# Other starting addresses for the operands of a sub-layer's products

## The chip, the cores and the metric

The kernel runs on one core of a Trainium2 chip, in one launch. The metric is the device time of an execution in microseconds (us); the median of three runs stands for a kernel. A profile is one more execution, recorded by the hardware profiler. "Busy" is the time in which an engine executes; the span is the time from the first to the last instruction on the core.

## The reference: what is computed

A two-layer diffusion backbone over 512 latent tokens and 256 context tokens, model width 1024, all in 32-bit floats. Each layer is a feed-forward half step, a token mixer (a short convolution in the first layer, grouped attention in the second), and another feed-forward half step:

```python
def swiglu(h, w_in, w_out):
    gate, up = jnp.split(h @ w_in, 2, axis=-1)
    return (jax.nn.silu(gate) * up) @ w_out
...
        h = norm_modulate(x_lat, norm_g[i, 2], m_lat[:, 2, 0], m_lat[:, 2, 1])
        x_lat = x_lat + MACARON_WEIGHT * m_lat[:, 2, 2] * swiglu(h, ffn_w_in[i, 1], ffn_w_out[i, 1])
        if not last:
            hc = norm_modulate(x_ctx, norm_g[i, 2], m_ctx[2, 0], m_ctx[2, 1])
            ...
    return rms_norm(x_lat, final_g)
```

`w_in` is 1024 x 5632 and `w_out` is 2816 x 1024. The second half step of the last layer (in the kernel `ffn(gp, 1, 2, "end", ...)`, the "last feed-forward sub-layer") works on the 512 latent tokens alone, since nothing reads the context tokens any more; all earlier sub-layers work on 768.

## The kernel before

**Splitting.** Every number that goes into a matmul is split into a high part (rounded by a ScalarE copy to the float type that TensorE takes at full pace) and a low part (what is left, a VectorE subtraction); `split`, L204 to L206. A product is then three matmuls, in this order: high weights by high operand (L876), high weights by low operand (L877), low weights by high operand (L878). This is the helper `mm3`. Every matmul loads its own weights of 128 x 128 beside the one before it.

**The seven products.** The input projection of a feed-forward sub-layer goes column by column: 22 columns of 128 gate and 128 up units. The first two columns are multiplied directly, gate and up, half of the tokens at a time (`directly`, L1106). The other 20 use Strassen's scheme on 2 x 2 blocks: tokens in two halves, the inner dimension in two halves, gate and up as the two rows. It takes seven block products M1 to M7 (`PRODUCTS`, L65) instead of eight, each over four chunks of 128 of the inner dimension: 4 x 3 matmuls (`product`, L1134). The weight combinations are formed by VectorE as they are needed (`add_product`, L384), split, and put into one of eight granules ahead of TensorE, or of some extra places.

**The operands T.** The moving operands of the products are eight pairs of tiles: the four blocks of the normalized input, B11, B21, B12, B22, and four combinations, T1 to T4. Each tile holds four rows of as many columns as there are tokens in a half: 384 in the earlier sub-layers, 256 in the last. The opening of a sub-layer (`opening`, L765) writes them: `early`, `parted` (L808) and `sum_parted` (L838), in program order on hooks between the matmuls of the sub-layer before and of the first columns. `t_tiles` (L748) makes the pair of a name.

**Slots.** Fourteen slots in SBUF, `T0` to `T13`, of 4 x 384 numbers (6144 bytes a partition), four of them with two more columns a row (386, for the first sub-layer's bias columns) and small tiles behind them, hold the T tiles in turn with other things: weight tiles, attention operands. A small tile `shift` of 24 numbers at the head of the constants and pads behind the wide slots set where the slots begin: in the program as built, every slot, every weight tile and every other matmul operand used here begins 96 bytes past a multiple of 256. In the last sub-layer a tile takes 4096 bytes of its slot, from the slot's first byte. Its slots are listed by

```python
LAST_T_SLOTS = {"B11": (0, 1), "B21": (2, 3), "B12": (6, 7), "T4": (6, 7), "T1": (8, 13), "B22": (9, 10), "T2": (11, 12), "T3": (4, 5)}
```

high part first. `geo` holds the halves' width and the slot table in force; before the last sub-layer it is set to 256 columns and this table (L1829).

**Order.** TensorE's and SyncE's instructions run in the order of the program text. The hooks, and in some regions a kept program order, set that of VectorE and ScalarE. Output products (`out_steps`) follow after every four columns: 512 columns wide, operands gh and gl.

Of the kernel before, what the change touches and what calls it, by code (L numbers as in the profile page):

```python
# [26 lines left out]
NH = NT // 2  # L27
# [47 lines left out]
HELD_AFTER_T = ((6, 7), (10, 11), (8, 9))  # L75

LAST_T_SLOTS = {"B11": (0, 1), "B21": (2, 3), "B12": (6, 7), "T4": (6, 7), "T1": (8, 13), "B22": (9, 10), "T2": (11, 12), "T3": (4, 5)}
LAST_F_SLOTS = {(0, 0): 4, (1, 0): 5, (0, 1): 11, (1, 1): 12}
HELD_AFTER_LAST_T = ((8, 13), (11, 12), (9, 10))
HELD_AFTER_HEADS = ((6, 7), (9, 10))  # L80
# [53 lines left out]
def backbone(ctx: ExitStack, tc: tile.TileContext, a: dict, out: bass.AP):  # L134
# [42 lines left out]
    vec, at = {}, 0  # L177
# [23 lines left out]
    def slot(n, shape, name, dt=F32R):  # L201
        return xp.tile([P, *shape], dt, name=name, tag=f"T{n}")
# [407 lines left out]
    hh, hl = [None] * KC, [None] * KC  # L610
# [125 lines left out]
    T, full = {}, {}  # L736
    geo = SimpleNamespace(tokens=TOKENS, half=NH, groups=BOTH, t_slots=T_SLOTS, f_slots=F_SLOTS)
# [8 lines left out]
        region.pop().close()  # L746

    def t_tiles(name, more=0):  # L748
        T[name] = [slot(n, [4, geo.half + more], f"t{name}{z}") for n, z in zip(geo.t_slots[name], "hl")]

    def t_split(name, src, ks, pinned=False):
        split(T[name][0][:, ks], T[name][1][:, ks], src[:, ks], pinned)
# [12 lines left out]
    def opening(i, s):  # L765
# [27 lines left out]
        def early(half):  # L793

            t_tiles(f"B{half + 1}1")
            off, n = geo.tokens[0]
            for k, (hi, lo) in enumerate(zip(*([t[:, k, :] for k in range(4)] for t in T[f"B{half + 1}1"]))):
                m = 4 * half + k
                scale = scl[:, m, LAT : LAT + 1]
                act.activation(hi, xs(m, off, n), AF.Copy, scale=scale)  # L800
                dve.scalar_tensor_tensor(out=lo, in0=xs(m, off, n), scalar=scale, in1=hi.bitcast(F32), op0=ALU.mult, op1=ALU.subtract)  # L801
# [6 lines left out]
        def parted(half, tok, p, which="both", more=0):  # L808
            name = f"B{half + 1}{tok + 1}"
            if p == 0 and which != "lo":  # L810
                t_tiles(name, more)
            hi, lo = T[name][0][:, PAIRS[p], : geo.half], T[name][1][:, PAIRS[p], : geo.half]
            src = full[half, tok][:, PAIRS[p]]
            if which != "lo":
                act.activation(hi, src, AF.Copy)
            if which != "hi":
                dve.tensor_tensor(out=lo, in0=src, in1=hi.bitcast(F32), op=ALU.subtract)
# [20 lines left out]
        def sum_parted(which, p, pinned=False):  # L838
            if p == 0:
                t_tiles(which)  # L840
            t_split(which, full[which] if which in full else full[0, 0], PAIRS[p], pinned)
# [984 lines left out]
    with tc.tile_pool(name="g1", bufs=1) as gp:  # L1826
        stage["ssq"] = lambda: gp.tile([P, NT], F32, name="ssq", tag="ssq")
        heads = attention(gp, 1, 1)
    geo.__dict__.update(tokens=HALVES, half=NL // 2, groups=((0, NL),), t_slots=LAST_T_SLOTS, f_slots=LAST_F_SLOTS)  # L1829
    op4 = opening(1, 2)  # L1830
# [79 lines left out]
```

## Time and profile before

| what | value |
|---|---|
| median of three runs | 2400.55 us (2399.58 to 2401.14) |
| the profiled execution | 2400.25 us |
| its span | 2398.4 us |
| mean granted TensorE clock | 0.998 |
| TensorE matmuls busy | 2377.5 us (99%), 14303 |
| weight loads busy | 2252.4 us (94%) |
| VectorE busy | 2031.9 us (85%) |
| ScalarE busy | 1166.3 us (49%) |
| last sub-layer, from its first opening writes to the end | about 2030 to 2398 us |

A matmul's recorded duration runs from its start until its last result is written, so the durations of successive matmuls overlap; the pace is the distance from one start to the next.

### The profile page before, as it was taken

Reading aid. Unit: us, or ns where it says so; the run is one execution under the profiler, and the core shown is the slowest. Engines: PE = TensorE matmul, PEld = TensorE weight load, DVE = VectorE, ACT = ScalarE, POOL = GpSimd, SP = SyncE. Lnnn points to the kernel's source line nnn. Section 1 sums busy time; section 2 is a strip of 40 time slices with the busy share of each in tenths; the row PEclk is TensorE's granted clock in tenths of the full one; section 3 lists DMA queues with packets and bytes.
Section 4 is the critical chain, followed back from the end, with each engine's and each line's share of the span. In section 5 each row is a group of like instructions: output and inputs, shape, how many; then the busy total and the mean of one; then the engine's idle time right before and its main releaser. Section 6 shows DMA issues by size and latency. Waiting matters only on the chain.

```text
span 2398.4 us, 37639 instructions
## 1 busy us (share of the span) xinstructions
PE 2377.5 (99%) x14303; PEld 2252.4 (94%) x14303; DVE 2031.9 (85%) x4018; ACT 1166.3 (49%) x2198; POOL 135.4 (6%) x256
## 2 busy tenths in 40 slices
PE   9999999999999999999999999999999999999998
PEld 6999999999999999999999999999998889999998
DVE  6989989978988888888877988788778987987777
ACT  5634334355535553443435544343356776555555
POOL 0001111100000001000000001101100000000000
PEclk9999999999999999999999999999999999999999
DMA  9234444430334123323432144444441101233331
GB/s 337 86 113 139 129 127 131 129 115 27 107 105 132 40 70 116 119 95 117 128 105 67 51 130 129 142 139 120 136 132 54 45 10 58 70 121 96 99 106 62
DMA packets 93062, 253.71 MB, mean 106 GB/s; under 512 B 10320, under 2 KB 18640, under 8 KB 92880
## 3 DMA queue, kind: packets, MB, share of 16 engines
q1 hardware_dynamic: 71984, 183.65, 23.7%
q0 software_dynamic: 20352, 67.12, 9.5%
q8 instruction: 112, 1.84, 0.3%
q14 instruction: 70, 0.57, 0.1%
q10 hardware_dynamic: 544, 0.52, 0.1%
HBM read 249.16 MB, written 2.10 MB: 105 GB/s over the span
## 4 chain that ended last, share of the span: by engine, by line
PE 91%; DVE 4%; ACT 3%; DMA 1%; issue 1%; SPq 0%; DVEq 0%; ACTq 0%
PE ps_A L876 16%; PE ps_A L877 16%; PE ps_A L878 16%; PE ps_C L877 11%; PE ps_C L878 11%; PE ps_C L876 11%; PE ps_B L878 3%; PE ps_B L877 3%; PE ps_B L876 3%; PE ps_T L1557 1%; DVE f L778 0%; DMA ada<-in_ada_w 0%; DMA raw<-in_ffn_w_in 0%; ACT pr L1540 0%; PE ps_O L878 0%
## 5 line engine op out<-in xcount | busy, mean ns | idle before, releaser
L205 ACT ACTIVATE w<-raw 128x512 fp32r<-128x512 f32 (+1 forms) x862 | 522.4, 619 | 713.6 <-PE ps_A L878 222.6
L206 DVE TENSOR_TENSOR w<-raw,w 128x512 fp32r<-128x512 f32 (+1 forms) x862 | 574.0, 678 | 120.0 <-ACT w L205 106.3
L525 POOL DMA_DIRECT2D aw<-in_ada_t x240 | 129.4, 539 | 1367.0 <-DVE mods L546 968.5
L389 DVE TENSOR_TENSOR raw<-raw,raw 128x512 f32<-128x512 f32 x264 | 181.4, 688 | 10.0 <-DMA raw<-in_ffn_w_in 6.0
L877 PE MATMUL ps_C<-gl,w 128*128 128x512 f32 (+1 forms) x548 | 188.3, 344 | 0.0
L876 PE MATMUL ps_C<-gh,w 128*128 128x512 f32 (+1 forms) x548 | 188.1, 343 | 0.0
L878 PE MATMUL ps_C<-gh,w 128*128 128x512 f32 (+1 forms) x548 | 188.0, 343 | 0.0
L876 PE MATMUL ps_A<-gh,w 128*128 128x512 f32 (+1 forms) x540 | 185.5, 344 | 0.6 <-DVE x L944 0.6
L877 PE MATMUL ps_A<-gl,w 128*128 128x512 f32 (+1 forms) x540 | 185.6, 344 | 0.0
L878 PE MATMUL ps_A<-gh,w 128*128 128x512 f32 (+1 forms) x540 | 185.4, 343 | 0.0
L546 DVE CUSTOM_DVE_ANT_0 ps_S<-aw,silu_row,packed 128x512 f32<-128x512 f32 x208 | 156.8, 754 | 2.1 <-DMA aw<-in_ada_t 0.8
L546 DVE CUSTOM_DVE_ANT_0 ps_S<-aw,silu_row,mods 128x512 f32<-128x512 f32 x208 | 156.7, 753 | 1.0
L944 DVE SCALAR_TENSOR_TENSOR x<-ps_C,gat,x 128x512 f32<-128x512 f32 (+1 forms) x158 | 99.4, 630 | 44.0 <-PE ps_C L878 43.6
L876 PE MATMUL ps_A<-tB11h,w 128*128 128x384 f32 (+1 forms) x400 | 129.6, 324 | 0.2 <-ACT tB11h L800 0.2
L877 PE MATMUL ps_A<-tB11l,w 128*128 128x384 f32 (+1 forms) x400 | 129.3, 323 | 0.2 <-DVE tB11l L801 0.2
L878 PE MATMUL ps_A<-tB11h,w 128*128 128x384 f32 (+1 forms) x400 | 129.2, 323 | 0.0
L878 PE MATMUL ps_C<-tB22h,w 128*128 128x384 f32 (+2 forms) x376 | 121.6, 323 | 0.0
L877 PE MATMUL ps_C<-tB22l,w 128*128 128x384 f32 (+2 forms) x376 | 121.4, 323 | 0.0
L876 PE MATMUL ps_C<-tB22h,w 128*128 128x384 f32 (+2 forms) x376 | 121.3, 323 | 0.0
L944 DVE SCALAR_TENSOR_TENSOR x<-ps_A,gat,x 128x512 f32<-128x512 f32 (+1 forms) x162 | 101.7, 637 | 16.6 <-PE ps_A L878 16.4
L876 PEld LDWEIGHTS ps_A<-gh,w 128*128 128x128 f32 x540 | 102.2, 189 | 14.1 <-issue 1.0
L878 PEld LDWEIGHTS ps_C<-gh,w 128*128 128x128 f32 x548 | 103.8, 189 | 12.3
(486 smaller groups left out, 6938.7 us busy)
## 6 DMA issues: line engine op xcount, KB each, us to landing
raw<-in_ffn_w_in SPq DMA_DIRECT2D x170, 512.0 KB, 3.7
aw<-in_ada_t POOLq DMA_DIRECT2D x240, 256.0 KB, 2.9
raw<-in_ffn_w_out SPq DMA_DIRECT2D x80, 512.0 KB, 3.9
raw<-in_conv_w_in SPq DMA_DIRECT2D x24, 512.0 KB, 3.6
ada<-in_ada_w SPq DMA_DIRECT2D x28, 256.0 KB, 5.3
raw<-in_attn_w_qkv SPq DMA_DIRECT2D x12, 512.0 KB, 4.7
raw<-in_ada_w SPq DMA_DIRECT2D x8, 512.0 KB, 6.6
silu_row<-in_crow POOLq DMA_DIRECT2D x8, 512.0 KB, 4.1
```

The source lines that it names most:

```text
L205: hi = act.activation(dsth, src, AF.Copy)
L206: lo = dve.tensor_tensor(out=dstl, in0=src, in1=dsth.bitcast(F32), op=ALU.subtract)
L389: dve.tensor_tensor(out=quad(o), in0=quad(x), in1=quad(y), op=ALU.subtract)
L525: nc.gpsimd.dma_start(w, a["ada_t"][t, kh, j])
L546: ins = dve.tensor_tensor_reduce(out=junk, in0=w, in1=silu_row[kh][:, v, :], scale=1.0, scalar=total if kh else ada_b[:, i, hm // 2, col : ...
L876: pe.matmul(ps, wh, xh, start=first, stop=False, **kw)
L877: pe.matmul(ps, wh, xl, start=False, stop=False, **kw)
L878: pe.matmul(ps, wl, xh, start=False, stop=last, **kw)
L944: dve.scalar_tensor_tensor(out=x, in0=p[:, o - off : o - off + w], scalar=gat[:, m, v : v + 1], in1=x, op0=ALU.mult, op1=ALU.add)
L1557: pe.transpose(pt[:, c, :], pr[:, (c0 + c) * P : (c0 + c + 1) * P], ident)
```

## The change

The T tiles of the last sub-layer begin later in their slots: the high part's tile 32 numbers (128 bytes) and the low part's 16 numbers (64 bytes) after the slot's first byte. The tile is made flat, that much longer, and the view that the rest of the program uses leaves the first numbers out. Rows follow each other as before, 256 numbers each. Slots, instructions and their order, and the tiles of all other sub-layers (`geo.half == NH`) stay as they are.

```diff
 LAST_T_SLOTS = {"B11": (0, 1), "B21": (2, 3), "B12": (6, 7), "T4": (6, 7), "T1": (8, 13), "B22": (9, 10), "T2": (11, 12), "T3": (4, 5)}
+LAST_T_STARTS = (32, 16)
 LAST_F_SLOTS = {(0, 0): 4, (1, 0): 5, (0, 1): 11, (1, 1): 12}
...
     def t_tiles(name, more=0):
-        T[name] = [slot(n, [4, geo.half + more], f"t{name}{z}") for n, z in zip(geo.t_slots[name], "hl")]
+        if geo.half == NH:
+            T[name] = [slot(n, [4, geo.half + more], f"t{name}{z}") for n, z in zip(geo.t_slots[name], "hl")]
+            return
+        T[name] = []
+        for n, z, at in zip(geo.t_slots[name], "hl", LAST_T_STARTS):
+            t = slot(n, [at + 4 * geo.half], f"t{name}{z}")
+            T[name].append(t[:, at:].rearrange("p (k c) -> p k c", k=4))
```

## The prediction

> **What bounds the kernel now.** I read the page's busy times and its chain first, then a table of busy times by stretch around the last feed-forward sub-layer, then single matmuls in order of time.
>
> ```profile
> PE 2377.5 (99%) x14303; PEld 2252.4 (94%) x14303; DVE 2031.9 (85%) x4018; ACT 1166.3 (49%) x2198; POOL 135.4 (6%) x256
> PE 91%; DVE 4%; ACT 3%; DMA 1%; issue 1%; SPq 0%; DVEq 0%; ACTq 0%
> ```
>
> TensorE is busy 99% of the span and holds 91% of the chain that ended last. A busy TensorE need not be at its peak, so the question is at what pace the matmuls follow each other where the changed tiles are read. The table (columns: stretch, its length, busy us and instructions of PE, PEld, DVE, ACT and POOL, granted clock, DMA share, GB/s):
>
> ```profile
> 2036.00:2062.50 26.50, 26.00 (x212) 25.27 (x211) 24.25 (x50) 17.44 (x37) 0.00 (x0) 1.00 0.09 32
> 2062.50:2087.00 24.50, 22.89 (x140) 19.97 (x139) 24.07 (x45) 12.15 (x29) 0.00 (x0) 1.00 0.25 86
> 2087.00:2300.00 213.00, 213.00 (x1520) 201.71 (x1520) 176.14 (x319) 115.38 (x235) 0.00 (x0) 1.00 0.34 108
> ```
>
> Until about 2087 us the sub-layer opens behind VectorE (24.07 of 24.50 us busy in the second row). From 2087 on TensorE has no idle time at all (213.00 of 213.00), at a granted clock of 1.00. There every nanosecond of the pace counts.
>
> Starts of single matmuls (columns: start us, duration us, engine, line, output<-inputs), 256, 384 and 512 columns wide:
>
> ```profile
> 2144.73 0.28 PE L876 MATMUL ps_B<-tB21h,w 128*128 128x256 f32 x1
> ...
> 2145.93 0.28 PE L877 MATMUL ps_A<-tT3l,w 128*128 128x256 f32 x1
> ```
>
> ```profile
> 571.05 0.33 PE L876 MATMUL ps_B<-tB12h,w 128*128 128x384 f32 x1
> ...
> 573.13 0.33 PE L876 MATMUL ps_B<-tB12h,w 128*128 128x384 f32 x1
> ```
>
> ```profile
> 2199.82 0.39 PE L877 MATMUL ps_A<-gl,w 128*128 128x512 f32 x1
> ...
> 2202.09 0.39 PE L878 MATMUL ps_A<-gh,w 128*128 128x512 f32 x1
> ```
>
> Ten matmuls of 256 columns lie between the first pair: 1.20 us, 120 ns each. Twelve of 384: 2.08 us, 173.3 ns each. Ten of 512: 2.27 us, 227 ns each. From 256 to 384 columns the step is 53.3 ns for 128 columns, 0.417 ns a column; what is left over is 13.3 ns at each width (120 - 106.7, 173.3 - 160, 227 - 213.3). So each matmul takes its columns plus a constant 13.3 ns, the time of 32 columns, that is of 128 bytes of a moving row. The stretch from 2087 to 2300 agrees: of its 1520 matmuls 288 are the output products of 512 columns (six groups of 48) and 1232 are of 256, and 288 x 0.227 + 1232 x 0.120 = 213.2 us against 213.00.
>
> ```profile
> L877 PE MATMUL ps_C<-gl,w 128*128 128x512 f32 x48 | 18.7, 390 | 0.0
> ```
>
> This 13.3 ns is the only thing in the stage that the address of a moving operand could touch.
>
> **The change part by part.** No instruction, wait or DMA is added, taken away or put elsewhere; nothing is moved past a queue. The tiles T of the last sub-layer keep their slots, and what changes is where inside its slot a tile begins: high parts 128 bytes further, low parts 64. In the program as built every slot begins 96 bytes past a multiple of 256, and so does every weight tile. Afterwards high parts begin 224 past it, low parts 160. Modulo 128 the high parts stay at 96 and the low parts go to 32; modulo 64 nothing changes.
>
> *The writes.* Eight tile pairs, two halves each: 16 ScalarE copies and 16 VectorE subtractions write at the new addresses. The trace has the same writes with rows 8 bytes out of step (the first sub-layer's tB12 and tB22 have two more columns a row) beside rows in step (tB11, tB21):
>
> ```profile
> L817 DVE TENSOR_TENSOR tB11l<-f,tB11h 128x768 fp32r<-128x768 f32 x2 | 1.9, 960 | 1.0 <-ACT tB11h L815 1.0
> L817 DVE TENSOR_TENSOR tB12l<-f,tB12h 128x768 fp32r<-128x768 f32 x2 | 1.9, 956 | 0.1
> L815 ACT ACTIVATE tB11h<-f 128x768 fp32r<-128x768 f32 x2 | 1.7, 848 | 0.1
> L815 ACT ACTIVATE tB12h<-f 128x768 fp32r<-128x768 f32 x2 | 1.7, 846 | 0.2 <-DVE f L789 0.2
> ```
>
> 960 against 956 and 848 against 846 ns: at most 4 ns apart in either direction, so 32 writes are worth -0.1 to +0.1 us. I take 0. If the cover were gone (they feed the opening, which VectorE sets) that 0.1 us would be the whole cost.
>
> *The reads.* The sub-layer has 22 columns, 2 of them multiplied directly and 20 by seven products of 4 x 3 matmuls: 20 x 84 = 1680 matmuls of 256 columns read the T tiles, and the direct columns 192 more. The 192 and about one column's 84 run before 2087 us, where VectorE sets the pace and a TensorE that is faster only waits; about 1600 count. One nanosecond on each is 1.6 us.
>
> Does the pace depend on the address? Within what the trace holds, not on the slot. The tiles named below lie in different slots, at different distances from their weights and from their low parts, and each has the same median, 283 ns:
>
> ```profile
> L878 PE MATMUL ps_A<-tB11h,w x76: 282/283/283, 2036.8 to 2298.7; 128*128 128x256 f32 x76
> L876 PE MATMUL ps_C<-tB22h,w x64: 283/283/287, 2053.0 to 2297.0; 128*128 128x256 f32 x64
> L876 PE MATMUL ps_A<-tT3h,w x60: 283/283/283, 2081.2 to 2291.2; 128*128 128x256 f32 x60
> ```
>
> But all of them begin at 96 modulo 256. The one case off it is the first sub-layer's tB22, whose four rows begin 0, 8, 16 and 24 bytes further along:
>
> ```profile
> 121.21 0.33 PE L876 MATMUL ps_C<-tB22h,w 128*128 128x384 f32 x1
> 121.38 0.33 PE L877 MATMUL ps_C<-tB22l,w 128*128 128x384 f32 x1
> ...
> 122.25 0.33 PE L876 MATMUL ps_C<-tB22h,w 128*128 128x384 f32 x1
> 122.42 0.33 PE L877 MATMUL ps_C<-tB22l,w 128*128 128x384 f32 x1
> 122.59 0.34 PE L878 MATMUL ps_C<-tB22h,w 128*128 128x384 f32 x1
> 122.77 0.34 PE L876 MATMUL ps_C<-tB22h,w 128*128 128x384 f32 x1
> ...
> 123.12 0.34 PE L878 MATMUL ps_C<-tB22h,w 128*128 128x384 f32 x1
> 123.30 0.34 PE L876 MATMUL ps_A<-tB11h,w 128*128 128x384 f32 x1
> ```
>
> These twelve take 2.09 us against 2.08 in step, 0.8 ns more a matmul; the row at 16 bytes goes at 0.17 us a matmul, and the last, at 24 bytes, takes 0.53 us for three (177 ns each, 3.4 above 173.3). So the address does matter, at the scale of some bytes. The matmul that follows another width also leaves the pace:
>
> ```profile
> 182.91 0.28 PE L876 MATMUL ps_A<-gh,w 128*128 128x256 f32 x1
> 183.03 0.28 PE L877 MATMUL ps_A<-gl,w 128*128 128x256 f32 x1
> 183.14 0.28 PE L878 MATMUL ps_A<-gh,w 128*128 128x256 f32 x1
> 183.26 0.28 PE L876 MATMUL ps_A<-gh,w 128*128 128x256 f32 x1
> ...
> 2245.35 0.40 PE L876 MATMUL ps_C<-gh,w 128*128 128x512 f32 x1
> 2245.58 0.40 PE L877 MATMUL ps_C<-gl,w 128*128 128x512 f32 x1
> 2245.82 0.39 PE L878 MATMUL ps_C<-gh,w 128*128 128x512 f32 x1
> ...
> 2246.51 0.39 PE L878 MATMUL ps_A<-gh,w 128*128 128x512 f32 x1
> ```
>
> The first three after 182.91 need 0.35 us, not 0.36; the five from 2245.35 to 2246.51 need 1.16, not 1.135 (5 ns more each). After a few both fall back to the constant pace. I read that as follows: the start of a read is held to some regular beat, and the beat is short enough that 256, 384 and 512 columns all end on the same place in it. A shift by a whole number of beats then changes nothing. All widths seen are multiples of 128 columns, so the rows leave open whether the beat is 128 bytes (32 columns, the 13.3 ns) or a part of it, 64 or 32; a beat of 32 or 64 bytes makes both new starts neutral. That rows 16 and 24 bytes out already differ (0.52 us for three, from 122.25 to 122.77, against 0.53) speaks for a beat well below 128 bytes. That is inference, and it is where I choose.
>
> Bounds for the reads: from below, two of three matmuls lose half of the constant (6.7 ns), 1600 x 2/3 x 6.7 = -7.1 us; from above the same with the other sign, +7.1 us, which is the size of the dearest row out of step (3.4 ns on each, 5.4 us) and of the disturbed 512s (5 ns, 8 us). Near to neither, I take 0, as for all slots.
>
> Sum: 0 (instructions) + 0 (writes) + 0 (reads) on the profiled execution's 2400.25 us (span 2398.4 and 1.85 around it), which is 0.3 us under the median of the runs, 2400.55. **Forecast: 2400.3 us, no change**, its own range 2397 to 2404.
>
> The Trainium skill, TensorE: Matmul & The Clock Gate, section Back-to-back issue gap, gives N / 2.4 + 2.5 ns between matmuls, 109 ns for 256 columns where this trace shows 120 in each of some thousand; by that rule 10.8 ns of the 13.3 is not owed to the matmul itself, and if the new starts removed that, 1600 x 10.8 = 17 us, the sum would be 2383. The trace nowhere reaches that pace at 256 columns, and the section's own sustained figures lie off the formula too; it only makes the last case of the first rival below less absurd.
>
> **The rivals.** *Faster, by a half turn.* If the beat is 128 bytes, a matmul over a low part begins 64 bytes off from the high one before it, and the next high one again. The 32 columns' wait would become 16 in two of each three (high to low and low to high; high to high, with the next weights, keeps 32). -7.1 us: 2393.2. VectorE could follow: it is busy 19.42 of 20.00 us where products run, and would have 19.26, but makes weight parts up to eight ahead and has 13.33 of 20.00 in the output stretches.
>
> ```profile
> 2100.00:2120.00 20.00, 20.00 (x169) 20.00 (x168) 19.42 (x38) 14.21 (x32) 0.00 (x0) 1.00 0.41 136
> 2180.00:2200.00 20.00, 20.00 (x103) 17.13 (x102) 13.33 (x23) 6.74 (x14) 0.00 (x0) 1.00 0.25 79
> ```
>
> For it: 13.3 ns is exactly 128 bytes' worth. Against it: the same wait is met whether the next read is of the high or the low part, and the rows off by 8 bytes did not gain. Should the whole constant go (weights and moving rows, now both at 96 modulo 256, getting out of each other's way), 1600 x 13.3 = 21 us: 2379.
>
> *Slower, by the same half turn.* The mechanism is the wait of a read for its place in the beat, at each change from high to low part and back. If the least time between reads is above 16 columns, the half turn comes too early, the read waits for the next one, and 32 becomes 48: +6.7 ns on two of three, from 2087 us on, where TensorE has no slack: 2407.4. It decides as soon as that least time exceeds 6.7 ns. For it: the return from the row 24 bytes out to one in step (0.18 us between the last two starts of that list) is dear, not cheap. Against it: the 0.11 us steps after 182.91 show that less than 13.3 is possible.
>
> *The change does not do what it says*: the tiles could have been given other room, with new waits between tiles. The slots' room is fixed by their first and largest tile, 6144 bytes, and the shifted tile needs 4224, so this is unlikely, and the time is the forecast's.
>
> **How the numbers follow.** Forecast 0.44 and the last rival 0.03, both without change; faster by the half turn 0.26, by the whole constant 0.06; slower 0.21. About 0.2% (4.8 us) is what a measurement of this kernel can tell from no change; both half turns lie beyond it. Faster 0.32, within 0.47, slower 0.21. The range takes in both half turns and a microsecond or two beside them, and leaves the whole constant out: 2391 to 2408.5.
>
> **What would show it.** Matmuls of 256 columns at 120 ns in the products of the last sub-layer, and 1520 of them with the 512s between the same two points, prove the forecast; 113 ns on two of three the faster rival, 127 the slower one. The writes should keep their durations. I am wrong if the pace inside a high, low, high triple is uneven, or if the median of 283 ns moves; the pace before 2036 us must be as it was.

## The result, and the profile after

The changed kernel takes 2395.86 us (median, 2395.14 to 2396.78) against 2400.34 us (2399.42 to 2401.14) for the kernel before beside it: a ratio of 0.9982, 95% interval 0.9976 to 0.9989. That is 4.5 us less, a gain that stands clear of the scatter and is just under the 0.2% (4.8 us) that the prediction counts as no change.

The table of busy times by stretch, after (columns as before: stretch, length, PE, PEld, DVE, ACT, POOL, granted clock, DMA share, GB/s). Rows four and five are 30 us each inside the first two blocks of products (a block is the products of four columns, between two groups of output products), the last row is 15 us of output products:

```profile
2036.00:2062.50 26.50, 25.96 (x213) 25.21 (x213) 24.32 (x51) 17.55 (x37) 0.00 (x0) 1.00 0.10 32
2062.50:2087.00 24.50, 22.64 (x139) 19.74 (x138) 24.27 (x46) 12.32 (x29) 0.00 (x0) 1.00 0.26 86
2087.00:2300.00 213.00, 213.00 (x1548) 201.77 (x1547) 178.17 (x323) 117.33 (x238) 0.00 (x0) 1.00 0.34 111
...
2089.00:2119.00 30.00, 30.00 (x254) 30.00 (x254) 29.03 (x58) 20.36 (x45) 0.00 (x0) 1.00 0.39 125
2145.00:2175.00 30.00, 30.00 (x259) 30.00 (x258) 28.19 (x54) 20.43 (x43) 0.00 (x0) 1.00 0.33 102
...
2125.00:2140.00 15.00, 15.00 (x68) 12.43 (x67) 10.57 (x17) 3.95 (x7) 0.00 (x0) 1.00 0.07 26
```

The last three of these stretches before:

```profile
2089.00:2119.00 30.00, 30.00 (x253) 30.00 (x252) 28.94 (x58) 20.06 (x46) 0.00 (x0) 1.00 0.38 123
2145.00:2175.00 30.00, 30.00 (x253) 30.00 (x252) 28.11 (x53) 19.68 (x41) 0.00 (x0) 1.00 0.28 86
...
2125.00:2140.00 15.00, 15.00 (x68) 12.40 (x67) 10.37 (x16) 3.79 (x6) 0.00 (x0) 1.00 0.06 22
```

Between 2087 and 2300 us TensorE is busy in all of 213.00 us as it was, at the same clock, and gets through 1548 matmuls instead of 1520. The opening before 2087 us is nearly as it was (at 2087 us the changed kernel is 0.3 us ahead). A count takes in the matmuls cut by either edge, so the pace is (length + duration of one) / count: (30 + 0.28) / 259 = 116.9 ns in the second block of products, 119.2 in the first, and (15 + 0.39) / 68 = 226.3 ns for the output products, which have not changed.

The groups by line and shape between 2087 and 2300 us, after (matmuls, then busy us, mean ns of one, idle time before them):

```profile
L883 PE MATMUL ps_A<-tT3h,w 128*128 128x256 f32 x60 | 16.9, 282 | 0.0
L884 PE MATMUL ps_A<-tT3l,w 128*128 128x256 f32 x60 | 16.8, 280 | 0.0
L885 PE MATMUL ps_A<-tT3h,w 128*128 128x256 f32 x60 | 16.7, 278 | 0.0
...
L883 PE MATMUL ps_C<-gh,w 128*128 128x512 f32 x48 | 18.7, 389 | 0.0
```

The 283 ns of every product matmul have become 282, 280 and 278 in the mean, by the place in the triple; the 512-column ones keep their 389. The profile models the ends of matmuls, so the pace is read from the starts. Single matmuls, after (start, duration):

```profile
2144.43 0.28 PE L883 MATMUL ps_B<-tB21h,w 128*128 128x256 f32 x1
...
2146.18 0.29 PE L883 MATMUL ps_A<-tT3h,w 128*128 128x256 f32 x1
```

Fifteen matmuls in 1.75 us, 117 ns each. Taken over the starts of all product matmuls after 2087 us, the pace is 117.4 ns, against 119.98 before: 2.6 ns on about 1600 matmuls is 4.2 us of the 4.5. That it arises there and nowhere else shows when one follows the same matmul in both traces:

| start in the trace of before, us | 140 | 1847 | 2056 | 2159 | 2260 | 2357 | 2388 |
|---|---|---|---|---|---|---|---|
| after less before, us | -0.12 | -0.10 | -0.17 | -1.00 | -2.64 | -4.34 | -4.45 |

The writes, before and then after (VectorE's subtraction and ScalarE's copy of one of the moved pairs; behind the first bar the busy us and the mean ns of one):

```profile
L206 DVE TENSOR_TENSOR tT4l<-fT,tT4h 128x512 fp32r<-128x512 f32 x2 | 1.3, 682 | 0.0
L205 ACT ACTIVATE tT4h<-fT 128x512 fp32r<-128x512 f32 x2 | 1.2, 620 | 0.0
```

```profile
L207 DVE TENSOR_TENSOR tT4l<-fT,tT4h 128x512 fp32r<-128x512 f32 x2 | 1.3, 692 | 0.0
L206 ACT ACTIVATE tT4h<-fT 128x512 fp32r<-128x512 f32 x2 | 1.3, 630 | 0.0
```

10 ns is the largest difference among the eight pairs, 0.3 us if all 32 writes had it.

So the address of the moving operand does set the pace. The experiments ask which address, or which distance between addresses.

### The profile page after: what moved, and what is told of

Read it like the earlier page. It is cut to its first block, busy times and chain, and to the rows that moved or that the text cites. A ratio compares the mean times of both kernels' runs of the same rounds, so it can differ in the third digit from the quotient of the medians.

```text
span 2394.0 us, 37639 instructions
## 1 busy us (share of the span) xinstructions
PE 2372.9 (99%) x14303; PEld 2247.7 (94%) x14303; DVE 2031.4 (85%) x4018; ACT 1168.2 (49%) x2198; POOL 135.4 (6%) x256
## 4 chain that ended last, share of the span: by engine, by line
PE 90%; DVE 4%; ACT 3%; DMA 1%; issue 1%; SPq 0%; DVEq 0%; ACTq 0%
PE ps_A L883 16%; PE ps_A L884 16%; PE ps_A L885 16%; PE ps_C L883 11%; PE ps_C L884 11%; PE ps_C L885 11%; PE ps_B L885 3%; PE ps_B L883 3%; PE ps_B L884 3%; PE ps_T L1564 1%; DMA ada<-in_ada_w 0%; DVE f L785 0%; DVE w L207 0%; DMA raw<-in_ffn_w_in 0%; ACT pr L1547 0%
```

## The experiments

Each kernel is the changed one with the edit shown. Most were run once, beside a run of the kernel before on the same chip (2400.48 us for the first four, 2399.78 for the next four, 2400.15 for the ninth to eleventh, medians where there were several); two that looked like improvements were run repeatedly. "Pace" is the mean distance from one start to the next among the product matmuls after 2087 us; distances above 145 ns (at most six in a run) are left out.

The theories: the prediction's own (a beat of 64 bytes, so nothing changes) has already lost, since something did. H: what counts is that high and low parts differ by 64 bytes. A: what counts is where the moving rows themselves lie. R: what counts is where they lie against the weights, which are loaded for the next matmul while one runs; the first expectations call it W, and there each matmul goes by its own rows' distance alone. In the kernel before, every distance in these products is 0 modulo 256.

### Low parts alone

```diff
-LAST_T_STARTS = (32, 16)
+LAST_T_STARTS = (0, 16)
```

> Starts (0, 16): low parts 64 bytes in, high parts at the slot's first byte. Theory H (what counts is how far the low part begins from the high part modulo 128 bytes, here 64 as in the changed kernel): the mean pace of the product matmuls is 117.4 ns as in the changed kernel, about 4.5 us below the kernel before. Theory W (what counts is each part's distance from the weights modulo 256 bytes; high parts are back on the weights' phase, low parts 64 off): only the low parts' matmuls change, about a third of the gain, 1.5 us. Theory of the prediction (64 bytes are whole beats): 120 ns and no change; it has already fallen with the changed kernel unless the 128 bytes did it.

2396.04 us, pace 117.77 ns, even within the triple and through the whole stretch:

```profile
2087.00:2300.00 213.00, 213.00 (x1544) 201.65 (x1543) 177.72 (x323) 116.67 (x237) 0.00 (x0) 1.00 0.34 111
```

One third of the reads, moved by 64 bytes, brings nearly the whole gain (4.4 us). That is what H expected; W expected a third of it, so each matmul does not go by its own distance alone.

### High parts alone

```diff
-LAST_T_STARTS = (32, 16)
+LAST_T_STARTS = (32, 0)
```

> Starts (32, 0): high parts 128 bytes in, low parts at the slot's first byte. Theory H: high and low differ by 128, which is 0 modulo 128, so 120 ns and no change (within 0.5 us). Theory W: high parts are half of 256 bytes off the weights, two of three matmuls change, about two thirds of the gain, 3 us.

2399.62 us, pace 119.86 ns, 1523 matmuls in the same stretch. The three distances of a triple are no longer equal (117.7, 120.5 and 121.4 ns), but add up to 359.6, almost the 360 of before. The 128 bytes of the high parts give next to nothing by themselves; the 0.9 us of the single run is within the scatter (0.2 us by the pace), and the 3 us that W expected did not come.

### Both parts by 64 bytes

```diff
-LAST_T_STARTS = (32, 16)
+LAST_T_STARTS = (16, 16)
```

> Starts (16, 16): both parts 64 bytes in. Theory H: no difference between high and low, 120 ns and no change. Theory W: all three matmuls of a triple are 64 bytes off the weights; if the low parts' distance did the work in the changed kernel, a gain of 4.5 us or more. It also tells whether the place modulo 128 bytes counts by itself.

2396.32 us, pace 117.78 ns:

```profile
2087.00:2300.00 213.00, 213.00 (x1544) 201.67 (x1543) 177.95 (x323) 116.52 (x237) 0.00 (x0) 1.00 0.34 111
```

High and low parts are in step here, as they were before, and the pace is that of the low parts moved alone. H, which expected 120 ns, falls.

### Low parts by 32 bytes, and both by 32

```diff
-LAST_T_STARTS = (32, 16)
+LAST_T_STARTS = (0, 8)
```

> Starts (0, 8): low parts 32 bytes in. Theory H with the half turn as its best point: something between 117.4 and 120 ns, 1 to 4 us gained. If only the phase modulo 64 bytes counts for a read by itself: low parts now begin 0 modulo 64 instead of 32, and the pace goes another way than in all other runs. Theory W: a third of the matmuls change, by an unknown amount.

2395.78 us, pace 117.09 ns, 1551 matmuls in the stretch.

```diff
-LAST_T_STARTS = (32, 16)
+LAST_T_STARTS = (8, 8)
```

> Both parts of the T tiles 32 bytes in (starts (8, 8)), weights as before. Theory R with any distance from the weights breaking the 120 ns: between 117 and 118 ns, 2395 to 2397 us. If the low part alone at 32 bytes gained only because the two parts differ: 120 ns, 2400 us.

2395.05 us, pace 116.68 ns, 1556 matmuls. By the pace, a shift of 32 bytes does a little more than one of 64; the times come from single runs and don't tell.

### All weight granules by 64 bytes instead

The T tiles are back at the first byte of their slots, and the eight granules that hold weights for TensorE lie 64 bytes further, in the whole kernel.

```diff
-LAST_T_STARTS = (32, 16)
+LAST_T_STARTS = (0, 0)
...
         if where is None:
+            if not n:
+                wp.tile([P, 16], F32, name="padw", tag="padw", bufs=1)
             t = wp.tile([P, 2, D // 2], F32R, name=f"w{n}", tag="w", bufs=GRANULES)
+            if not n:
+                wp.tile([P, 48], F32, name="padx", tag="padx", bufs=1)
```

> T tiles at their slots' first byte (starts (0, 0)); instead the eight granules that hold most weight tiles, of all sub-layers, begin 64 bytes further (160 past a multiple of 256, all other tiles as before). Theory R (what counts is the moving operand's place against that of the weights that are loaded beside it, modulo 128 bytes; the run with both parts 64 in gave 117.8 ns without any difference between high and low): the products of the last sub-layer go at 117.8 ns as with both parts moved, and the earlier sub-layers' 384-column matmuls gain about 2 ns each too, some 15 to 25 us in all: 2376 to 2386 us. Theory A (what counts is the moving operand's own place modulo 128 bytes, wherever the weights are): 120 and 173.3 ns as before, 2400 us.

2394.38 us, pace 113.36 ns in all three of a triple. Stretches, and groups between 2087 and 2300 us:

```profile
2145.00:2175.00 30.00, 30.00 (x267) 30.00 (x266) 28.60 (x55) 20.64 (x44) 0.00 (x0) 1.00 0.31 96
...
2125.00:2140.00 15.00, 15.00 (x66) 12.10 (x65) 10.42 (x17) 3.80 (x6) 0.00 (x0) 1.00 0.15 52
```

```profile
L888 PE MATMUL ps_C<-gl,w 128*128 128x512 f32 x48 | 19.0, 396 | 0.0
...
L887 PE MATMUL ps_A<-tT4h,w 128*128 128x256 f32 x61 | 16.8, 276 | 0.0
```

267 matmuls in 30 us (113.4 ns) where the moving rows have not moved at all: A falls. The output products pay: 66 in 15 us (233 ns) instead of 68, 396 ns instead of 389. The other sub-layers show the same, by width: output products of 256 columns fall from 119.7 to 113.7 ns, products of 384 hardly move (173.4 before, 173.7 here), those of 512 rise from 227.8 to 233.1. So the gain of 15 to 25 us that R expected, most of it from the 384 columns, did not come: the paces bear R out, and its transfer to other widths failed. Following single matmuls through both traces, the kernel is 1.8 us late at 2056 us and 5.9 us early at 2388, so the last sub-layer has gained 7.7.

### Everything 64 bytes back

```diff
-LAST_T_STARTS = (32, 16)
+LAST_T_STARTS = (0, 0)
...
-SHIFT = 24
+SHIFT = 8
```

> T tiles at their slots' first byte; the tile at the head of the constants has 8 numbers instead of 24, so that every tile behind it, moving operands and weights alike, begins 64 bytes earlier. Theory R: nothing changes against one another, 120 ns and 2400 us. Theory A: all moving operands are now 32 modulo 128, as the T tiles were with both parts 64 in, so 117.8 ns in the last sub-layer and a gain of 2 ns a matmul in the earlier ones: 2376 to 2386 us.

2400.25 us, pace 119.97 ns:

```profile
2087.00:2300.00 213.00, 213.00 (x1520) 201.71 (x1520) 176.13 (x319) 115.37 (x236) 0.00 (x0) 1.00 0.33 108
```

The same 1520 matmuls as before, with every address another one. Addresses by themselves do nothing.

### Weights and both parts by 64 bytes

The weight edit above, with

```diff
-LAST_T_STARTS = (32, 16)
+LAST_T_STARTS = (16, 16)
```

> Both parts of the T tiles 64 bytes in (starts (16, 16)) and the weight granules 64 bytes further as well. Theory R: the products of the last sub-layer are back in step with their weights, 120 ns there, while the other matmuls that take weights from the granules keep what moving the weights alone gives; so this run is slower than that one by about 4 us. Theory A: 117.8 ns in the last sub-layer, 2396 us.

2405.19 us, pace 119.96 ns:

```profile
2150.00:2180.00 30.00, 30.00 (x253) 30.00 (x252) 27.53 (x53) 20.29 (x42) 0.00 (x0) 1.00 0.34 106
```

253 in 30 us, (30 + 0.28) / 253 = 119.7 ns. Two shifts, each of which made the products faster, undo each other. What is left is a loss: 2.2 us in the earlier sub-layers, whose weights have moved too, and some 2.7 us in the last, where the output products go at 233.4 ns. Of the theories named, these three runs leave R: the pace goes by the distance between the moving rows and the weights.

The distance has a sign. Rows 64 bytes past the weights went at 117.8 ns, rows 64 bytes short of them (weights moved) at 113.4. If the distance counts modulo 256, rows moved by 192 bytes must do the same as weights moved by 64; if modulo 128, they must do what rows moved by 64 do.

### Both parts by 192, 128 and 224 bytes

```diff
-LAST_T_STARTS = (32, 16)
+LAST_T_STARTS = (48, 48)
```

> High and low parts of the last sub-layer's T tiles both begin 192 bytes inside their slots; everything else stays, so that the products' moving rows stand 192 bytes past their weights modulo 256, which is the distance of the kernel with all weights moved 64 bytes on (113.4 ns a matmul of 256 columns there). Theory R256 (the pace goes by the distance between a moving row and the weights, modulo 256 bytes): 113.4 ns in all three of a triple, 6.6 ns on some 1600 matmuls, -10.6 us, 2389 to 2391 us, faster than both kernels, and the output products of 512 columns stay at 226.7 ns. Theory R128 (the same, modulo 128): 192 is 64, so 117.8 ns as with both parts at 64 bytes, about 2396 us. A theory in which the weights' own address made the gain: 120 ns and 2400 us, or 117.8 ns by the moving row's own place.

2395.05 us (median of 11, 2394.06 to 2395.93), ratio 0.9978, interval 0.9969 to 0.9987; pace 116.92 ns. Neither 113.4 nor 117.8, but both:

```profile
2089.00:2119.00 30.00, 30.00 (x267) 30.00 (x266) 29.15 (x59) 20.30 (x46) 0.00 (x0) 1.00 0.39 130
2145.00:2175.00 30.00, 30.00 (x257) 30.00 (x257) 28.06 (x54) 20.49 (x43) 0.00 (x0) 1.00 0.33 106
...
2125.00:2140.00 15.00, 15.00 (x68) 12.43 (x67) 11.79 (x18) 4.43 (x7) 0.00 (x0) 1.00 0.11 40
```

The first block of products goes at 113.33 ns throughout (267 in 30 us), the later ones at 117.78 (257), with the same tiles at the same addresses. The stretches from 2053 us on, ahead of 2087 us, went at 117.78 as well (the first of the direct columns, at 2037 us, at 113.7), until TensorE had to wait for weights several times:

```profile
2082.57 0.28 PE L885 MATMUL ps_A<-tT3h,w 128*128 128x256 f32 x1
2083.59 0.39 PE L883 MATMUL ps_C<-tT1h,w 128*128 128x256 f32 x1 [0.74 <-ACT w L206]
...
2086.75 0.38 PE L885 MATMUL ps_A<-tT2h,w 128*128 128x256 f32 x1 [0.23 <-DVE w L207]
```

The last of these waits (0.23 us, at 2086.75) is followed by 113.33 ns without a break to the end of the block; the later blocks follow output products without a wait. The expectation of 2389 to 2391 us failed, and with it the idea that the distance alone gives the pace.

```diff
-LAST_T_STARTS = (32, 16)
+LAST_T_STARTS = (32, 32)
```

> High and low parts both 128 bytes inside their slots. Theory R128: 128 is 0, the pace stays 120.0 ns flat, 1520 matmuls in the stretch from 2087 to 2300 us, 2400 us. Theory R256: 128 is a distance of its own; the pace may be anything between 113 and 123 ns and need not be flat; high part alone at 128 bytes went at 119.9 ns but unevenly within its triples, so I expect 119 to 121 ns, 2399 to 2402 us, which this run alone would not separate from R128 unless the steps are uneven.

2399.36 us, pace 119.75 ns: 118.7 in the first block of products and 119.98 in the others, with triples of 117.6, 119.8 and 121.9 ns. The first block and the uneven triples are not those of distance 0, so 128 bytes are not quite the same as none; the time hardly tells.

```diff
-LAST_T_STARTS = (32, 16)
+LAST_T_STARTS = (56, 56)
```

> High and low parts both 224 bytes inside their slots, that is 32 bytes before the place of the weights modulo 256. Theory R256: between 120 ns (distance 0) and 113.4 (64 bytes before): 116 to 117 ns, 2394 to 2396 us. Theory R128: 224 is 96, which is not measured; it is as far from 0 as 32, where the pace was 116.7 ns. If the gain comes in steps and not by degrees, 120 or 113.4 ns.

2396.94 us, pace 118.34 ns, the same in every block of products. Expected were 116 to 117: 32 bytes short of the weights is worse than 32 past them (116.7).

### Both parts and the output products' operands by 192 bytes

Once more the 192 bytes, and gh and gl of the last sub-layer moved as far, so that every moving row of that sub-layer stands against its weights as it did with the weights moved. For the products nothing differs from the run with 192 bytes but what goes ahead of them.

```diff
-LAST_T_STARTS = (32, 16)
+LAST_T_STARTS = (48, 48)
...
-                t = gp.tile([P, per, width], F32R, name=f"g{z}{f}", tag=tags(z, f // per))
+                if geo.half != NH:
+                    t = gp.tile([P, 64 + per * width], F32R, name=f"g{z}{f}", tag=tags(z, f // per))
+                    t = t[:, 48 : 48 + per * width].rearrange("p (q c) -> p q c", q=per)
+                else:
+                    t = gp.tile([P, per, width], F32R, name=f"g{z}{f}", tag=tags(z, f // per))
```

> Both parts of the T tiles of the last sub-layer 192 bytes inside their slots, as in the run that took 113.33 ns in its first stretch of products and 117.78 in the others; and now the operands gh and gl of its output products are 192 bytes further too, so that in the whole last sub-layer every moving row stands where it stood, against its weights, with all weights moved by 64 bytes. Theory entry (two rhythms are possible at this distance, and what runs ahead of a stretch of products decides which one it falls into): the output products of 512 columns take 233.3 ns instead of 226.7, the products behind them fall into 113.33 ns everywhere as with the moved weights; -6.65 ns x 1580 = -10.5 us, +6.6 ns x 384 = +2.5 us, and the 192 last matmuls of 256 columns at 113.7 instead of 119.9 ns, -1.2 us: 9.2 us under before, 2391 us. Theory place (the weights' own address, or the rows' own, made 113.33 ns there): the products stay at 117.78 in all stretches but the first, and the time is that of the run before with 2.5 us more for the output products and up to 1.2 less at the end, 2395 to 2398 us.

2391.87 us (median of 5, 2391.58 to 2392.63) against 2400.37, ratio 0.9966, interval 0.9952 to 0.9979; pace 113.35 ns:

```profile
2087.00:2300.00 213.00, 213.00 (x1576) 199.96 (x1576) 178.83 (x327) 117.91 (x243) 0.00 (x0) 1.00 0.35 114
...
2145.00:2175.00 30.00, 30.00 (x267) 30.00 (x267) 28.56 (x55) 20.77 (x44) 0.00 (x0) 1.00 0.34 109
...
2125.00:2140.00 15.00, 15.00 (x66) 12.10 (x65) 11.70 (x18) 4.44 (x7) 0.00 (x0) 1.00 0.12 42
```

The output products are slower, 66 in 15 us, and every block of products behind them now goes at 113.33 ns (267), as with the weights moved; so what ran ahead decides between the two paces of this distance. Moving the output products' operands slowed these and made the products after them faster; whether by their slower pace or by their own distance is not told apart.

That 192 bytes past do what 64 short do fits a count modulo 256 and modulo 128 alike. Against 128 speak two runs. Rows 64 past came through the same waits ahead of 2087 us (0.74, 0.48 and 0.22 us), and stayed at 117.78 ns behind them, where rows 192 past went over to 113.33 (267):

```profile
2089.00:2119.00 30.00, 30.00 (x257) 30.00 (x256) 29.11 (x58) 20.38 (x46) 0.00 (x0) 1.00 0.39 128
```

And rows 128 past have uneven triples, where distance 0 has even ones in all three runs that have it.

The gain of the version with both moved, 8.5 us, is nearly twice that of the change, and 0.7 under the 9.2 that the theory of the entry gave; the trace has 1576 matmuls where the changed kernel had 1548. This version is faster than both kernels.

## Why the prediction was right, and where it was wrong

**The outcome.** The forecast of no change within 0.2% held by a hair (4.5 us of 4.8), and the time lies inside the wide range of 2391 to 2408.5. It lies outside the forecast's own range of 2397 to 2404, and the forecast's reason for zero was wrong. That "no change" held is luck: the pace did move, against the reason given, and only its small size kept the gain under 4.8 us.

**What bounds the kernel** held: the pace of TensorE from 2087 us on, and nothing ahead of it. All of the gain arises behind 2056 us, and a 2.6 ns change of pace on some 1600 matmuls gives the measured size.

**The writes** were costed at 0 with 0.1 us to either side. Their means changed by at most 10 ns, 0.3 us in all if every write had it: the bound was too tight, the term right, since the opening is not later than before.

**The reads** are the step that failed: "a beat of 32 or 64 bytes makes both new starts neutral". Half of its reasoning stood up. With rows and weights in step, the steady paces at all three widths are whole numbers of one beat of 6.67 ns (16 columns, 64 bytes of a moving row; below). But from a beat of 64 bytes it doesn't follow that a shift by 64 bytes is neutral: the next weights are loaded while a matmul runs (PEld is busy 201.71 of 213.00 us), the rows stand at some distance from the weights, and a change of this distance changed the pace, in the changed kernel to 17 5/9 beats. The rows quoted from before could not have shown that: every T tile stood at the same distance from its weights. The prediction saw this ("all of them begin at 96 modulo 256") and still took several slots with equal medians as a sign for neutrality. By both signs that it set itself the step is wrong: the median of 283 ns moved to 283, 279 and 278 by the place in the triple, and the pace inside a triple is uneven (118.1, 117.9 and 116.1 ns from the first, second and third start to the next).

**Faster, by a half turn** had the sign, and neither the mechanism nor the size. It expected 113 ns on two of three matmuls from the 64 bytes between high and low part; measured were 116 to 118 on all three, and with both parts in step the gain was nearly the same (4.2 us). Its bound of -7.1 us was too small for what shifts of this kind can do: 113.33 ns in all three, 6.7 ns x 1580 = 10.6 us for the products alone.

**The whole constant** was given a chance of 0.06, and its reason, "weights and moving rows getting out of each other's way", names the distance that the three runs with weights, everything, and both moved single out. Only the size was off: at most half of the 13.3 ns went in any run, not all of it. By the Trainium skill, TensorE: Matmul & The Clock Gate, section Back-to-back issue gap, the formula for the gap between single matmuls comes to 109 ns at 256 columns; the fastest steady pace of any run here is 113.33, so it isn't reached.

**Slower, by the same half turn** did not happen to the products. The size that it named, 6.7 ns a matmul, is what the 512-column matmuls lost with the weights moved (226.7 to 233.3).

**VectorE could follow**, as was said: in the fastest run it is busy 28.56 of 30 us in the products, and TensorE has no idle time from 2087 to 2300 us.

## What to carry to other kernels

Where TensorE is the bound and each matmul loads its own weights, the start of the moving operand against the weights' start is a parameter worth trying: some tens of bytes moved the pace of 256-column matmuls by up to 5.5%, at no cost in instructions. Try it by width and on the whole sequence, since the same distance helps 256 columns, hardly touches 384 and costs 512, and since the pace that a run of matmuls falls into depends on what ran ahead of it. And a trace in which all operands share one alignment says nothing about alignment, however many rows agree.

## What the runs showed of the hardware

*A beat of 6.67 ns.* In a steady run of matmuls the mean distance of the starts is a whole number of this beat or a simple fraction more, to some 0.05 ns:

| pace, ns | beats a matmul | where |
|---|---|---|
| 113.33 | 17 | rows 64 bytes short of the weights, or 192 past, 256 columns |
| 116.67 | 17 1/2 | both parts 32 past |
| 117.04 | 17 5/9 | the changed kernel; low parts 32 past |
| 117.78 | 17 2/3 | low parts or both 64 past; 192 past in most blocks |
| 118.33 | 17 3/4 | both 224 past |
| 120.00 | 18 | distance 0; high parts or both 128 past |
| 173.33 | 26 | 384 columns, distance 0 |
| 226.67, 233.33 | 34, 35 | 512 columns, distance 0; 64 short |

The prediction's 13.3 ns over the columns' own time are thus two beats; the fastest runs leave one. A matmul of 256 columns without any gap would take 16 beats, and no run came near it. The whole numbers carry this reading; ninths would fit many a pace to 0.05 ns. And the beat is a unit of the mean, not a grid on which every start falls: with both parts 32 past, the starts follow each other at 116 and 117 ns throughout, and in the changed kernel's second block the distances run from 112 to 123 ns. High parts alone (119.86 ns) fit no simple fraction.

*One distance, two rhythms.* With rows 192 bytes past the weights, 17 and 17 2/3 beats both occur in one execution, each for hundreds of matmuls without a break. What ran ahead decides: behind output products of 34 beats the products fell into 17 2/3, behind output products of 35 beats, and behind one of several waits, into 17. The run with the weights moved shows both as well, 117.8 ns in its first direct columns at 2039 us and 113.4 from 2087 us on. The changed kernel has two rhythms too, 118.9 ns in its first block and 117.0 in the later ones.

*What stays open.* That the distance between moving rows and weights counts is shown; why is not. That the two reads get into each other's way at the memory is one explanation that fits, and was only argued. It was not tried to make the products without their weight loads, which would have tested it. Nor is it known what in the output products selects the rhythm (their last start within the beat, or something that lasts longer), nor whether still other distances, or different ones for high and low parts, give 113.33 ns without slower output products.
